# A two-layer decoder trunk on one core: trailing sums by scans, and second weight parts by a negation and an adding transfer

## The chip, the core and the metric

The kernel runs on one core of a Trainium2 chip. The number that counts is the device time of one execution in microseconds (us), median of three runs. Five engines take part, each with its own queue that is worked off in order: PE (TensorE, the matmuls), DVE (VectorE), ACT (ScalarE), POOL (GpSimd) and SP (SyncE, which here only issues transfers).

## The reference

The trunk has two layers, 1024 channels and 1024 tokens, all in float32. Each layer is a token mixer and then a squared-ReLU MLP with 4096 hidden channels; ahead of each stands an RMSNorm with a scale and a shift that come from a conditioning vector, and a last norm ends the trunk. Layer 0 mixes with a gated recurrence. Layer 1, which the change concerns, mixes with trailing means:

```python
def pool_mixer(h, w_pool, pool_scale):
    counts = jnp.arange(1, s + 1, dtype=jnp.float32)
    for g, win in enumerate((2, 4, 8, 16)):          # 4 groups of 256 channels
        xg = hf[..., g * 256:(g + 1) * 256]
        cs = jnp.cumsum(xg, axis=1)
        cs_lag = jnp.pad(cs, ((0, 0), (win, 0), (0, 0)))[:, :s]
        mean = (cs - cs_lag) / jnp.minimum(counts, float(win))[None, :, None]
        outs.append(mean - xg)
    mixed = jnp.einsum("bsgi,gij->bsgj", jnp.stack(outs, axis=2), w_pool)
    return mixed.reshape(bsz, s, 1024) * pool_scale

def sq_relu_mlp(h, w1, w2):
    u = jax.nn.relu(jnp.einsum("bsd,df->bsf", h, w1))
    return jnp.einsum("bsf,fd->bsd", u * u, w2)
```

## The kernel before

Channels lie on the 128 partitions, in eight blocks k; tokens lie along the free axis, in two halves of 512 (half 0 is `xa`, half 1 is `xb`). Matmuls take float32r operands. To keep float32 accuracy every operand is held in two parts that add up to it, and each product is three matmuls (`mm3`, L176 to L180): high weight by high data, high weight by low data, low weight by high data.

**Weights.** A unit of weights is a 128x1024 float32 tile that SP loads into `raw` (three buffers). `split_part` (L168 to L172) makes the two parts of a half unit of 512 columns: ACT copies it into the high part (L170), and DVE or POOL subtracts that from the raw tile (L171) into the low part. The tiles of parts come from a pool of eight, so ACT's copy for one half unit waits until PE has used the one eight places earlier. A half unit serves 12 matmuls.

**The MLP.** It is worked in chunks of 512 hidden channels, eight per layer. `f1` makes the hidden channels of a chunk, `f2` multiplies by the second matrix; `f2_fast` is a form of Strassen's for chunks of which both halves of tokens are there at once. After each block of `f1`, ACT takes the ReLU (L620), DVE squares it (L625), ACT casts the high part of `u` (L609) and DVE makes the low part (L610).

**The passage between the layers.** The second half of the program's work on the end of layer 0 and the start of layer 1 is written so that one half of the tokens has matmuls to do while the other half has norms and windows: `f1`, `f2` of the last chunk of layer 0 for half 0; then the windows of half 0 (`pool_windows`) beside the rest of `f2_fast` of chunk 6 and `f1` for half 1; `pool_mix` for half 0; `f2` of the last chunk for half 1, beside the norm for half 0's MLP (`ffn_norm`); the windows of half 1 beside layer 1's first chunk for half 0; `pool_mix` for half 1; and so on. Between these stand sums of squares over channels: ACT squares a block (L252), DVE (or POOL) adds it up (L253), PE sums over partitions (L262, `sm`), ACT takes the root (L265), DVE makes diagonals (`dg`, L274), PE spreads them (L276, `sm`). PE's rows for L262 and L276 stand at fixed places among its matmuls.

**The windows.** For each block k, DVE normalizes (`nt`, L880), ACT adds the shift into `hx` (L886), which holds 15 tokens of the half before ahead of its own 512. Blocks 0 and 1 (window 2) are a difference of neighbours (L939). The others add shifted copies, log2(window) times (`sums`, L900): blocks 2 to 5 on DVE, blocks 6 and 7 (window 16) on POOL, in advance. DVE then scales and subtracts (L907), mends the first 16 tokens of half 0 (L909, L910), ACT casts the high part (`ph`, L914) and DVE makes the low part (`pl`, L915). `pool_mix` multiplies these with the 256x256 matrices `w_p`, group by group, and DVE adds each block into x (L962).

The order of the instructions on each engine is set by a scheduler at build time, from the order in which the program is written, the dependencies and the free buffers; at run time each queue is strictly in that order. All temporaries of 512 tokens come from a pool of seven tiles (`tmp`), PSUM has six banks for products.

Of the kernel before, what the change touches and what calls it, by code (L numbers as in the profile page):

```python
# [15 lines left out]
P = 128  # L16
# [9 lines left out]
PAD = 15  # L26
W = PAD + H

# Columns of the packed per-channel vectors, eight columns (one per block of channels) each.
# [13 lines left out]
def trunk_kernel(ctx, tc, xT, vecs, wmod, w_k, w_in, w_y, w_g, w_out, w_p, w1, w2, outT):  # L43
# [16 lines left out]
    class Blocks:  # L60
        """Eight blocks of channels of one half of the tokens, in two slots"""
# [112 lines left out]
    def mm3(ps, unit, col, rh, rl, first, last):  # L174
        """ps += unit[:, col:col+128].T @ (rh + rl)"""
# [6 lines left out]
    def proj(unit, hh, hl):  # L182
        """One 128-row block of W.T @ h for one token half, K = 1024."""
# [11 lines left out]
    def mod_column(m, e, raw):  # L195
        """m[:, e] = raw @ cond"""
# [9 lines left out]
    def mod_steps():  # L206
        """The rest of the conditioning in small steps, taken between those of the other work."""
# [19 lines left out]
    def norm_scale(g, m, name):  # L227
        """g * (1 + scale)"""
# [5 lines left out]
    class SumSq:  # L234
        """Sums of squares of n tokens: up to three partial sums, added up by the tensor engine."""
# [19 lines left out]
    def rstd_bcast(ss, trace=None):  # L255
        """PSUM tile [P, n] with 1/sqrt(mean + eps) of every token on every partition."""
# [10 lines left out]
        # in two float32r parts on diagonals, whose sums over the partitions are on every partition  # L267
# [38 lines left out]
    # Six blocks of the input projection take the channels of the first half of the tokens  # L306
    # as the conditioning of each 128 of them is ready.
# [8 lines left out]
    def after(f, *args, **kw):  # L316
        """Issues behind what the last call on the same engine issued."""
# [7 lines left out]
    def column(dst, j, k, scale, first):  # L325
        """dst[:, k] = first + scale * (conditioning of channel block k)"""
# [16 lines left out]
    def prepare(q, part=0):  # L343
        """The float32r parts of the weights of two blocks of rows, or of one if q is 0"""
# [126 lines left out]
    # coefficient of the gate in log a: 8 * log_sigmoid(lambda)  # L471
# [17 lines left out]
    # log1p(z) = 2 s (1 + po)  # L489
# [11 lines left out]
    def gates(hd, unit, h):  # L501
        """RG-LRU of one head; its states take the place of its input."""
# [16 lines left out]
        for mi in range(2):  # L519
            b = 2 * hd + mi  # L520
            # a = exp(log a);  1 - a^2 = (1 + a^2) * tanh(-log a)
# [351 lines left out]
    def pool_windows(h, ss):  # L873
# [44 lines left out]
        for k in (6, 7):  # L918
            normed(k, hx16[:, k - 6, :])
# [193 lines left out]
```

## Time and profile before

| | |
|---|---|
| runs | 1798.16, 1798.73, 1800.46 us; median 1798.73 |
| span of the profiled execution, first to last instruction | 1797.3 us |
| PE busy | 1718.5 us (96%) |
| DVE busy | 1419.8 us (79%) |
| ACT busy | 913.7 us (51%) |
| POOL busy | 585.9 us (33%) |
| DMA engines, mean busy share | 26.9% |

The profile has no time of the profiled execution but its span; it stands 1.4 us under the median of the runs, and that much is taken to lie around it. Busy time counts an engine as busy while an instruction is in it; a PE row's duration is modelled, and the distance from one start to the next tells its pace. The granted clock (PEclk) is a share of full speed, where 1.0 is 2.4 GHz and 0.5 is 1.2 GHz.

### The profile page before, as it was taken

What the parts mean: (1) busy time and instruction counts of PE and PEld (TensorE: products, weight loads), DVE (VectorE), ACT (ScalarE), POOL (GpSimd) and SP (SyncE); (2) the same over time, 40 slices, a digit from 0 to 9 for tenths busy, and PEclk for the clock granted to TensorE, in tenths of its full rate; (3) what the DMA queues carried; (4) which work ended last, traced back from release to release, by engine and by line L of the source; (5) the groups of instructions that cost most, each with busy time, mean ns of one, the idle gap of its engine ahead of it and who ended that gap; (6) DMA issues with size and microseconds to landing.
All of it is one profiled execution on the core that took longest, in us unless ns stands there. A gap on an engine that the chain in (4) does not pass through costs nothing.

```text
span 1797.3 us, 20872 instructions
## 1 busy us (share of the span) xinstructions
PE 1718.5 (96%) x7510; PEld 1405.2 (78%) x7510; DVE 1419.8 (79%) x2124; ACT 913.7 (51%) x1558; POOL 585.9 (33%) x434
## 2 busy tenths in 40 slices
PE   6899989989999999999999988999999999999997
PEld 4687768778788888888888766788887787878787
DVE  8997866678888889898876897958787878686836
ACT  4588884255454444545454464445444444545422
POOL 5323341242322414151324655511322324041403
PEclk8999989989999999999999988999999999999999
DMA  9223314521424233242213221231202111121202
GB/s 363 73 84 109 136 47 142 162 83 59 136 70 134 73 115 106 94 126 73 83 58 106 81 72 59 83 105 51 70 33 71 36 59 52 42 61 46 71 13 94
DMA packets 47479, 158.76 MB, mean 88 GB/s; under 512 B 5008, under 2 KB 7440, under 8 KB 47376
## 3 DMA queue, kind: packets, MB, share of 16 engines
q1 hardware_dynamic: 47376, 157.43, 26.9%
q8 instruction: 59, 0.97, 0.2%
q14 instruction: 44, 0.36, 0.1%
HBM read 153.21 MB, written 4.19 MB: 88 GB/s over the span
## 4 chain that ended last, share of the span: by engine, by line
PE 62%; DVE 22%; ACT 5%; issue 5%; DMA 4%; POOL 2%; DVEq 0%; SPq 0%; ACTq 0%; POOLq 0%
PE mm L178 20%; PE mm L179 20%; PE mm L180 20%; DMA mb<-in_wmod 3%; DVE mb L197 2%; DVE xa L770 1%; DVE mw L323 1%; POOL xa L779 1%; DVE pw L900 1%; DVE xb L770 1%; DVE xca L439 1%; PE sm L262 1%; DVE hl L291 1%; DVE w_a_s L171 1%; DVE xcb L439 1%
## 5 line engine op out<-in xcount | busy, mean ns | idle before, releaser
L178 PE MATMUL mm<-hh,w_w 128*128 128x512 f32 x1024 | 401.4, 392 | 0.9 <-DVE xa L770 0.9
L180 PE MATMUL mm<-hh,w_w 128*128 128x512 f32 x1024 | 400.9, 392 | 0.0
L179 PE MATMUL mm<-hl,w_w 128*128 128x512 f32 x1024 | 400.6, 391 | 0.0
L779 POOL TENSOR_TENSOR xb<-xb,c 128x512 f32<-128x512 f32 x104 | 150.4, 1446 | 632.1 <-ACT c L774 564.4
L178 PEld LDWEIGHTS mm<-hh,w_w 128*128 128x128 f32 x1024 | 193.5, 189 | 42.8 <-DVE xa L770 2.7
L180 PEld LDWEIGHTS mm<-hh,w_w 128*128 128x128 f32 x1024 | 193.6, 189 | 40.3
L179 PEld LDWEIGHTS mm<-hl,w_w 128*128 128x128 f32 x1024 | 193.5, 189 | 40.0
L779 POOL TENSOR_TENSOR xa<-xa,c 128x512 f32<-128x512 f32 x104 | 160.3, 1542 | 145.1 <-ACT c L774 145.1
L774 ACT ACTIVATE c<-c,mod 128x512 f32<-128x512 f32 x104 | 75.3, 724 | 209.7 <-DVE c L800 119.8
L197 DVE SCALAR_TENSOR_TENSOR mb<-mb,cond 128x1024 f32<-128x1024 f32 x80 | 113.8, 1423 | 55.2 <-DMA mb<-in_wmod 54.6
L620 ACT ACTIVATE relu<-mm 128x512 f32<-128x512 f32 x128 | 76.2, 595 | 152.4 <-PE mm L180 143.6
L170 ACT CAST w_w<-raw_w 128x512 fp32r<-128x512 f32 x192 | 113.5, 614 | 63.2 <-PE mm L180 50.6
L171 DVE TENSOR_TENSOR w_w<-raw_w,w_w 128x512 fp32r<-128x512 f32 x136 | 130.5, 967 | 16.8 <-ACT w_w L170 16.7
L770 DVE SCALAR_TENSOR_TENSOR xa<-mm,mod,xa 128x512 f32<-128x512 f32 x156 | 112.9, 741 | 16.6 <-POOL xa L779 16.6
L171 POOL TENSOR_TENSOR w_w<-raw_w,w_w 128x512 fp32r<-128x512 f32 x56 | 83.5, 1498 | 71.6 <-ACT w_w L170 62.6
L179 PE MATMUL mm<-u,w_w 128*128 128x512 f32 (+1 forms) x224 | 81.4, 363 | 1.7 <-DVE u L610 1.7
L178 PE MATMUL mm<-u,w_w 128*128 128x512 f32 (+1 forms) x224 | 80.8, 364 | 1.7 <-ACT u L609 1.7
L180 PE MATMUL mm<-u,w_w 128*128 128x512 f32 (+1 forms) x224 | 81.0, 362 | 0.0
L178 PE MATMUL mm<-u,w_a_a 128*128 128x512 f32 x200 | 79.1, 396 | 1.9 <-DVE xa L770 1.0
L610 DVE TENSOR_TENSOR u<-usq,u 128x512 fp32r<-128x512 f32 x102 | 72.9, 715 | 8.5 <-ACT u L609 7.5
L770 DVE SCALAR_TENSOR_TENSOR xb<-mm,mod,xb 128x512 f32<-128x512 f32 x104 | 77.0, 741 | 2.6 <-PE mm L180 2.2
L179 PE MATMUL mm<-u,w_a_a 128*128 128x512 f32 x200 | 78.0, 390 | 0.0
(332 smaller groups left out, 4078.3 us busy)
## 6 DMA issues: line engine op xcount, KB each, us to landing
raw_w<-in_w SPq DMA_DIRECT2D x148, 512.0 KB, 3.6
mb<-in_wmod SPq DMA_DIRECT2D x80, 512.0 KB, 3.6
mw<-in_wmod SPq DMA_DIRECT2D x16, 512.0 KB, 9.6
raw_in<-in_w_in SPq DMA_DIRECT2D x8, 512.0 KB, 3.7
raw_y<-in_w_y SPq DMA_DIRECT2D x8, 512.0 KB, 3.6
raw_o<-in_w_out SPq DMA_DIRECT2D x8, 512.0 KB, 3.7
outT<-o SPq DMA_DIRECT2D x12, 256.0 KB, 2.4
xa<-in_xT SPq DMA_DIRECT2D x4, 512.0 KB, 5.4
```

What stands on the lines that cost most here:

```text
L170: S.copy(w[:, 0, 0:n], raw)
L171: (eng or V).tensor_sub(w[:, 1, 0:n], raw, w[:, 0, 0:n].bitcast(F32))
L178: PE.matmul(out=ps, lhsT=wh, rhs=rh, start=first, stop=False)
L179: PE.matmul(out=ps, lhsT=wh, rhs=rl, start=False, stop=False)
L180: PE.matmul(out=ps, lhsT=w[:, 1, c:c + P], rhs=rh, start=False, stop=last)
L197: V.scalar_tensor_tensor(raw, raw, 1.0, cond, op0=ALU.mult, op1=ALU.mult, accum_out=m[:, e:e + 1])
L439: V.scalar_tensor_tensor(o, xr[:, k:k + H], vcol(f"cw{k}", m), o, op0=ALU.mult, op1=ALU.add)
L610: eng.tensor_sub(u[n][:, 1, jj, :], src, u[n][:, 0, jj, :].bitcast(F32))
L620: S.activation(r, ps, AF.Relu)
L770: V.scalar_tensor_tensor(xb, ps, g[:, r + 4 * row:r + 4 * row + 1], xb, op0=ALU.mult, op1=ALU.add)
L774: S.activation(t, src, AF.Identity, scale=g[:, r + 4 * row:r + 4 * row + 1])
L779: G.tensor_add(xb, xb, t)
```

## The change

Two things are replaced, between the layers and at the start of layer 1.

**Trailing sums.** `sums` goes. `finish` runs one scan on DVE over a block: each element is the running sum plus the token that comes in, minus the token that leaves the window (add, then subtract). This holds for blocks 2 to 7, so that POOL no longer adds windows. The padding grows from 15 to 16 tokens. For half 0, ACT copies the last running sum of a block into `carry`, from which the scan of half 1 starts; the scaling by 1/window then writes over the running sums in place, so it stands behind that copy; and the first 16 tokens' products with 1/count are put in a small tile (`first`) ahead of it. The blocks are taken in the order 0 to 7, where blocks 6 and 7 went first.

**Second parts of weights.** `neg_part` replaces `split_part` for the units from `f1` of chunk 7, half 0, to `f2` of layer 1's chunk 0, half 1: 84 half units, 60 of whose low parts POOL made and 24 DVE. ACT copies the raw tile into the high part, then writes the negated high part into the low one; then POOL issues a transfer that reads the same half unit from memory again and adds it onto the low part.

```diff
+    def neg_part(raw, src, name):
+        w, n = split_tile(name), raw.shape[-1]
+        S.copy(w[:, 0, 0:n], raw)
+        S.activation(w[:, 1, 0:n], w[:, 0, 0:n].bitcast(F32), AF.Identity, scale=-1.0)
+        nc.gpsimd.dma_start(w[:, 1, 0:n], src, accum_op=ALU.add)
+        return w
+
     def split_unit(src, name, eng=None, drips=None):
         raw = load(src, name)
         drip(rate[0] if drips is None else drips)
+        if eng == "dma":
+            return [neg_part(raw[:, c:c + H], src[:, c:c + H], f"{name}_{c}") for c in (0, H)]
         return [split_part(raw[:, c:c + H], f"{name}_{c}", eng) for c in (0, H)]
...
-        def finish(k, hx, sm_, win):
-            d = tmp("pooled")
-            V.scalar_tensor_tensor(d, sm_, 1.0 / win, hx[:, PAD:W], op0=ALU.mult, op1=ALU.subtract)
+        def finish(k, hx):
+            win, d = WINDOWS[k // 2], tmp("pooled")
+            V.tensor_tensor_scan(d, hx[:, PAD:W], hx[:, PAD - win:W - win], 0.0 if h == 0 else carry[:, k:k + 1],
+                                 op0=ALU.add, op1=ALU.subtract)
             if h == 0:
-                V.tensor_mul(d[:, 0:16], sm_[:, 0:16], icnt[:, k // 2, :])
-                V.tensor_sub(d[:, 0:16], d[:, 0:16], hx[:, PAD:PAD + 16])
+                S.copy(carry[:, k:k + 1], d[:, H - 1:H])
+                first = mp.tile([P, 16], F32, tag="first", name="first", bufs=2)
+                V.tensor_mul(first, d[:, 0:16], icnt[:, k // 2, :])
+            V.scalar_tensor_tensor(d, d, 1.0 / win, hx[:, PAD:W], op0=ALU.mult, op1=ALU.subtract)
+            if h == 0:
+                V.tensor_sub(d[:, 0:16], first, hx[:, PAD:PAD + 16])
             split(k, d)
...
-        up = [split_unit(w_p[q], f"p{q}", G) for q in range(2)]
+        up = [split_unit(w_p[q], f"p{q}", "dma") for q in range(2)]
...
-    f1(0, 7, (0,))
-    f2(0, 7, (0,), sa)
+    f1(0, 7, (0,), eng="dma")
+    f2(0, 7, (0,), sa, eng="dma")
     side = pool_windows(0, sa)
-    f1(0, 7, (1,), eng=G, side=side)
+    f1(0, 7, (1,), eng="dma", side=side)
...
-    f2(0, 7, (1,), sb, eng=G, side=once(lambda: ffn_norm(1, 0, qa)))
+    f2(0, 7, (1,), sb, eng="dma", side=once(lambda: ffn_norm(1, 0, qa)))
     side = pool_windows(1, sb)
-    f1(1, 0, (0,), eng=G, side=side)
-    f2(1, 0, (0,), eng=G, side=side)
+    f1(1, 0, (0,), eng="dma", side=side)
+    f2(1, 0, (0,), eng="dma", side=side)
...
-    f1(1, 0, (1,), eng=G)
-    f2(1, 0, (1,))
+    f1(1, 0, (1,), eng="dma")
+    f2(1, 0, (1,), eng="dma")
```

Of the rest, `f2_weights_two` and `f1` of layer 1's chunk 1, half 0, change in the same way, and comments are gone, which shifts the line numbers.

The order on the engines moves at three places. First DVE, in the windows of half 0, one block of window 4 before (`pw` are the shifted sums, `usq` and `u` belong to the MLP's hidden channels):

```order
L880 SCALAR_TENSOR_TENSOR nt<-xa_82,amix_7305,sm 128x512
L883 MEMSET hx 128x15
L915 TENSOR_TENSOR pl_0_7953<-pooled,ph_0_7951 128x512
L900 TENSOR_TENSOR pw<-hx 128x526
L900 TENSOR_TENSOR pw<-pw 128x524
L907 SCALAR_TENSOR_TENSOR pooled<-pw,hx 128x512
L909 TENSOR_TENSOR pooled<-pw,icnt 128x16
L910 TENSOR_TENSOR pooled<-pooled,hx 128x16
L625 SCALAR_TENSOR_TENSOR usq<-mm,relu 128x512
```

The same place on DVE in the changed kernel; the scan is the row `pooled<-hx` of L905:

```order
L890 SCALAR_TENSOR_TENSOR nt<-xa_82,amix_7305,sm 128x512
L913 TENSOR_TENSOR pooled<-first,hx 128x16
L893 MEMSET hx 128x16
L905 SCALAR_TENSOR_TENSOR pooled<-hx 128x512
L918 TENSOR_TENSOR pl_0_7971<-pooled,ph_0_7969 128x512
L910 TENSOR_TENSOR first<-pooled,icnt 128x16
L911 SCALAR_TENSOR_TENSOR pooled<-pooled,hx 128x512
L635 SCALAR_TENSOR_TENSOR usq<-mm,relu 128x512
```

One scan stands where two shifted additions stood (three for window 8), and the scaling has moved behind ACT's copy into `carry`.

Then ACT, at the same stage, where the weights `w_p` of `pool_mix` are made between the steps of the windows, before:

```order
L170 CAST w_p_0_8297<-raw_p_8295 128x512
L888 COPY tail<-hx 128x15
L890 COPY hx<-hx 128x1
L886 ACTIVATE hx<-nt,mod_0_3550 128x512
L914 CAST ph_0_7951<-pooled 128x512
```

and in the changed kernel:

```order
L163 CAST w_p_0_8313<-raw_p_8311 128x512
L896 ACTIVATE hx<-nt,mod_0_3550 128x512
L908 COPY carry<-pooled 128x1
L164 ACTIVATE w_p_0_8313<-w_p_0_8313 128x512
L898 COPY tail<-hx 128x16
L163 CAST w_p_512_8317<-raw_p_8311 128x512
L164 ACTIVATE w_p_512_8317<-w_p_512_8317 128x512
L917 CAST ph_0_7969<-pooled 128x512
```

Each copy of weights has a negation (L164) behind it, and between two steps of the windows there are now two or three ACT instructions on weights where there was one.

Last PE, where the sum of squares for half 0's MLP norm is taken among the matmuls of `f2`, before (u is the hidden data, `w_w_0_7_1_512` the second half of `f2`'s second unit):

```order
L180 MATMUL mm<-u_8101,w_w_0_7_1_512_8503 128x512
L262 MATMUL sm<-ones,ssqf1aV 128x1 x4
L178 MATMUL mm<-u_8101,w_w_0_7_1_512_8503 128x512
L179 MATMUL mm<-u_8101,w_w_0_7_1_512_8503 128x512
L180 MATMUL mm<-u_8101,w_w_0_7_1_512_8503 128x512
```

and in the changed kernel, where the row stands behind the first unit:

```order
L190 MATMUL mm<-u_8098,w_w_0_7_0_512_8424 128x512
L272 MATMUL sm<-ones,ssqf1aV 128x1 x4
L188 MATMUL mm<-u_8097,w_w_0_7_1_0_8522 128x512
L189 MATMUL mm<-u_8097,w_w_0_7_1_0_8522 128x512
L190 MATMUL mm<-u_8097,w_w_0_7_1_0_8522 128x512
```

The row stood behind 39 matmuls of `f2` and stands behind 24. Else PE's order is the same but for a few rows that change places.

## Rows read from the trace of the kernel before

**Rows 1.** Windows: busy us (instructions) per engine, granted clock, DMA share, GB/s.
```profile
core 0: us, PE busy (x) PEld busy (x) DVE busy (x) ACT busy (x) POOL busy (x), PEclk, DMA share, GB/s
900.00:950.00 50.00, 50.00 (x222) 41.32 (x222) 40.53 (x60) 28.35 (x51) 16.51 (x12) 1.00 0.17 56
1005.00:1155.00 150.00, 131.51 (x523) 104.05 (x522) 132.53 (x177) 74.39 (x141) 88.69 (x60) 0.90 0.23 73
1200.00:1250.00 50.00, 50.00 (x222) 41.45 (x221) 38.16 (x66) 23.73 (x42) 3.12 (x3) 1.00 0.23 72
```

**Rows 2.** Waits of PE from 990 to 1160 us: who, total us, times, longest.
```profile
PE mm L178 <- DVE usq L625: 4.9, 1, 4.9
PE sm L262 <- DVE ssqn0bV L253: 4.4, 1, 4.4
PE mm L178 <- ACT ph L914: 1.9, 1, 1.9
PE mm L179 <- DVE u L610: 1.7, 1, 1.7
PE mm L178 <- DVE xa L962: 1.7, 2, 1.5
PE mm L178 <- ACT u L609: 1.7, 1, 1.7
PE sm L262 <- DVE ssqf1aV L253: 0.9, 1, 0.9
```

**Rows 3.** Timeline of PE: start, duration, instruction, [idle before, releaser].
```profile
1005.11 0.39 PE L178 MATMUL mm<-hh,w_w 128*128 128x512 f32 x1
1007.83 0.39 PE L178 MATMUL mm<-hh,w_w 128*128 128x512 f32 x1
...
1035.97 0.80 PE L178 MATMUL mm<-ph,w_p 128*128 128x512 f32 x1 [4.86 <-DVE usq L625]
1036.57 0.63 PE L179 MATMUL mm<-pl,w_p 128*128 128x512 f32 x1
1036.99 0.63 PE L180 MATMUL mm<-ph,w_p 128*128 128x512 f32 x1
...
1060.24 1.02 PE L262 MATMUL sm<-ones,ssqf1aV 128*128 128x1 f32 x8 [0.88 <-DVE ssqf1aV L253]
...
1063.53 0.39 PE L276 MATMUL sm<-dg,ones_r 128*128 128x512 f32 x1
...
1155.71 0.95 PE L262 MATMUL sm<-ones,ssqf1bV 128*128 128x1 f32 x8
```

**Rows 4.** Groups on DVE from 1010 to 1060 us: busy, mean ns, idle before.
```profile
L900 DVE TENSOR_TENSOR pw<-pw 128x524 f32<-128x524 f32 (+1 forms) x6 | 8.4, 1407 | 0.2
L253 DVE TENSOR_TENSOR ssqf1aV<-ssqf1aV,sq 128x512 f32<-128x512 f32 x7 | 6.6, 949 | 0.0
L962 DVE SCALAR_TENSOR_TENSOR xa<-mm,gp,xa 128x512 f32<-128x512 f32 x8 | 5.9, 742 | 1.2 <-PE mm L180 1.2
L915 DVE TENSOR_TENSOR pl<-pooled,ph 128x512 fp32r<-128x512 f32 x8 | 5.7, 726 | 0.2 <-ACT ph L914 0.2
L907 DVE SCALAR_TENSOR_TENSOR pooled<-pw,hx 128x512 f32<-128x512 f32 x6 | 5.4, 920 | 0.1
L900 DVE TENSOR_TENSOR pw<-hx 128x526 f32<-128x526 f32 x4 | 4.8, 1196 | 0.1
```

**Rows 5.** All instructions of one operation: durations min/median/max in ns, first and last start.
```profile
L536 DVE TENSOR_TENSOR_SCAN xca<-a,gate x8: 1196/1208/1218, 151.1 to 252.3; 128x512 f32<-128x512 f32 x8
L171 DVE TENSOR_TENSOR w_w<-raw_w,w_w x136: 673/693/1783, 456.6 to 1739.1; 128x512 fp32r<-128x512 f32 x136
L171 POOL TENSOR_TENSOR w_w<-raw_w,w_w x56: 1262/1346/2378, 348.8 to 1175.8; 128x512 fp32r<-128x512 f32 x56
```

**Rows 6.** Groups on ACT from 1000 to 1160 us, columns as in 4.
```profile
L170 ACT CAST w_w<-raw_w 128x512 fp32r<-128x512 f32 x37 | 22.5, 617 | 22.2 <-PE mm L180 20.3 <-issue 0.9 <-POOL pwork L900 0.9
L886 ACT ACTIVATE hx<-nt,mod 128x512 f32<-128x512 f32 x12 | 8.6, 722 | 1.7 <-DVE nt L880 1.7
L170 ACT CAST w_p<-raw_p 128x512 fp32r<-128x512 f32 x8 | 4.7, 615 | 2.4 <-PE mm L180 2.4
```

**Rows 7.** Transfers: issue on SP's queue (ns), and KB each, us to landing.
```profile
L99 SPq DMA_DIRECT2D raw_w<-in_w x96: 327/328/372, 330.6 to 1707.2; - x96
raw_w<-in_w SPq DMA_DIRECT2D x4, 256.0 KB, 2.8
kr<-in_w_k SPq DMA_DIRECT2D x1, 512.0 KB, 10.2
q1 hardware_dynamic: 47376, 157.43, 26.9%
```

**Rows 8.** Timeline of DVE around the windows of half 0: start, duration, instruction.
```profile
1005.98 1.41 DVE L880 SCALAR_TENSOR_TENSOR nt<-xa,amix,sm 128x512 f32<-128x512 f32 x2
...
1020.50 0.18 DVE L910 TENSOR_TENSOR pooled<-pooled,hx 128x16 f32<-128x16 f32 x1
...
1047.44 0.68 DVE L915 TENSOR_TENSOR pl<-pooled,ph 128x512 fp32r<-128x512 f32 x1
```

More of the change, by code (lines that the diff above doesn't have):

```diff
@@ L25 @@
 WINDOWS = (2, 4, 8, 16)
-PAD = 15
+PAD = 16
 W = PAD + H
@@ L744, in f2_weights_one, with f2_weights_two @@
         return {1: (wa, 0, (0, 0)), 3: (wa, 256, (1, 1)), 5: (wb, 256, "t1"), 6: (wb, 0, "t2"), 7: (wc, 0, "t3")}
-    def f2_weights_two(i, c, r, eng):
+    def f2_weights_two(i, c, r):
         raw = rawp.tile([P, D + 256], F32, tag="raw", name=f"raw_w2_{i}_{c}_{r}")[:, 0:H]
         nc.sync.dma_start(raw, w2[i, c, r, :, 256:768])
-        w = split_part(raw, "a12_a22", eng)
+        w = neg_part(raw, w2[i, c, r, :, 256:768], "a12_a22")
         return {2: (w, 0, (1, 0)), 4: (w, 256, "t4")}
@@ L890, in normed @@
                     S.copy(hx[:, PAD - 1:PAD], hx[:, PAD:PAD + 1])
-        def sums(hx, win, eng, work=None):
-            cur, n = hx, 0
-            step = 1
-            while step < win:
-                if work is None or 2 * step == win:
-                    nxt = tmp("pw", W)
-                else:
-                    nxt = work[:, step.bit_length() % 2, :]
-                eng.tensor_add(nxt[:, n + step:W], cur[:, n + step:W], cur[:, n:W - step])
-                cur, n = nxt, n + step
-                step *= 2
-            return cur[:, PAD:W]
-        def finish(k, hx, sm_, win):
-            d = tmp("pooled")
-            V.scalar_tensor_tensor(d, sm_, 1.0 / win, hx[:, PAD:W], op0=ALU.mult, op1=ALU.subtract)
-            if h == 0:
-                V.tensor_mul(d[:, 0:16], sm_[:, 0:16], icnt[:, k // 2, :])
-                V.tensor_sub(d[:, 0:16], d[:, 0:16], hx[:, PAD:PAD + 16])
+        def finish(k, hx):
+            win, d = WINDOWS[k // 2], tmp("pooled")
+            V.tensor_tensor_scan(d, hx[:, PAD:W], hx[:, PAD - win:W - win], 0.0 if h == 0 else carry[:, k:k + 1],
+                                 op0=ALU.add, op1=ALU.subtract)
+            if h == 0:
+                S.copy(carry[:, k:k + 1], d[:, H - 1:H])
[4 more added lines that the diff above has]
+                V.tensor_sub(d[:, 0:16], first, hx[:, PAD:PAD + 16])
             split(k, d)
@@ L915, in split @@
             V.tensor_sub(lo[:, k, :], d, hi[:, k, :].bitcast(F32))
-        hx16 = slot("hx", (2, W))
-        for k in (6, 7):
-            normed(k, hx16[:, k - 6, :])
-        work = slot("pwork", (2, W))
-        late = [(k, hx16[:, k - 6, :], sums(hx16[:, k - 6, :], 16, G, work), 16) for k in (6, 7)]
         hxs = {}
         def ahead(k):
-            if k < 6:
+            if k < NB:
                 hxs[k] = tmp("hx", W)
@@ L933, in pool_windows @@
         yield
-        for k in range(6):
+        for k in range(NB):
             ahead(k + 2)
@@ L941, in pool_windows @@
             else:
-                win = WINDOWS[k // 2]
-                finish(k, hx, sums(hx, win, V), win)
-            if k == 4:
-                for args in late:
-                    finish(*args)
-            if k != 0:
+                finish(k, hx)
+            if k % 2 or k == 2:
                 yield
@@ L976, in trunk_kernel @@
     f2_fast(0, 6, Ahead([partial(f2_weights_one, 0, 6, r, V) for r in range(4)]), (1, 5, 6, 3, 7))
-    f1(0, 7, (0,))
-    f2(0, 7, (0,), sa)
+    f1(0, 7, (0,), eng="dma")
+    f2(0, 7, (0,), sa, eng="dma")
     side = pool_windows(0, sa)
-    f2_fast(0, 6, Ahead([partial(f2_weights_two, 0, 6, r, G) for r in range(4)]), (2, 4), side)
-    f1(0, 7, (1,), eng=G, side=side)
+    f2_fast(0, 6, Ahead([partial(f2_weights_two, 0, 6, r) for r in range(4)]), (2, 4), side)
+    f1(0, 7, (1,), eng="dma", side=side)
     for _ in side:
@@ L991, in trunk_kernel @@
     pool_mix(1, pooled[1], qb)
-    f1(1, 1, (0,), eng=G, side=once(lambda: ffn_norm(1, 1, qb)), fast="in turn")
-    f1(1, 0, (1,), eng=G)
-    f2(1, 0, (1,))
+    f1(1, 1, (0,), eng="dma", side=once(lambda: ffn_norm(1, 1, qb)), fast="in turn")
+    f1(1, 0, (1,), eng="dma")
+    f2(1, 0, (1,), eng="dma")
     ahead = Ahead(jobs(1, 1, 7))
```

## The prediction

> **What bounds the kernel now.** I read the busy times in long windows first. Before and after the passage between the layers PE is busy all the time at full clock: 50.00 of 50 us with 222 matmuls, twice [rows 1]. Only the passage, 1005 to 1155 us, falls out: 131.5 of 150 us busy, granted clock 0.90, while DVE is busy 132.5, ACT 74.4 and POOL 88.7 us [rows 1]. So a change can win in this passage alone, and I first ask how much is lost there. At full pace PE starts a matmul every (1007.83 - 1005.11) / 12 = 0.227 us [rows 3]. From the first matmul of `f1` at 1005.11 to the sum for half 1's MLP norm at 1155.71 [rows 3] there are 504 of them in the order (21 groups of 24), 114.2 us, and with two sums and two spreads of about 1.5 us together each, 117.3. The trace takes 150.6. **Lost: 33.3 us**, and no change in this passage can win much more.
>
> The waits of PE tell to whom it is lost: 17.2 us in seven rows, nearly all on DVE or on ACT steps that DVE releases [rows 2]. The other half is pace: after the 4.86 us wait at 1036, matmuls start 0.42 us apart, not 0.227 [rows 3]; the engine has dropped from 2.4 to 1.2 GHz after idling. A wait of 0.88 us in front of the sum at 1060.24 is the small kind [rows 2, 3]. Hence a wait that vanishes also takes its slow stretch along.
>
> The reason is a DVE backlog. In the windows of half 0 DVE runs from 1006 to 1048.1 with hardly an idle moment [rows 4, 8], and PE stands in front of `pool_mix` because the squares of `f1`, queued between windows, free their PSUM banks late (the 4.9 us row, released by `usq`) [rows 2]. The later waits (sums `ssqf1a`, `ssqn0b`, then `u`, `ph`) are the same backlog carried on.
>
> **The scans, and DVE freed from POOL.** Removed for half 0 on DVE: ten shifted additions, 8.4 + 4.8 = 13.2 us [rows 4]. Added: six scans. The kernel's own scans of 128x512 take 1.21 us [rows 5], so 7.3 us; they mix other operations, and the nearest other rows are 0.69 (one plain pass) and 1.78 (the slowest subtraction) [rows 5], which bounds the six at 4.1 and 10.7. I take 1.21, the same instruction. POOL's 16 additions of windows go too, and its subtractions of weights with them. That matters to DVE: the same subtraction takes 0.69 at the median and up to 1.78 [rows 5], and in the windows L907 stands at 0.92 and the adds of squares at 0.95 [rows 4]. At 0.69 the six L907 give 1.4 back, and the small mending steps, the differences and L915 about as much twice over, 4.2 us in all (below 0 there is no reason; 0 if the slow ones had another cause). DVE also no longer has four x updates (L962, 0.74 each) and one add of squares (0.69), 3.7 us, ahead of the last `pl`, since these stand behind it in the new order. So the last `pl` comes at 1048.1 - 13.2 + 7.3 - 4.2 - 3.7 = 1034.3. PE reaches `pool_mix` at 1005.11 + 96 x 0.227 = 1026.9, and its last group after 36 more, 1035.0. It need not wait. The banks are free as well, as the squares move up with the windows.
>
> **The copy into `carry`.** The scaling in place now waits for an ACT copy of one column, and DVE's whole queue waits behind it. ACT is at most one weight pair behind, 0.62 + 0.72 us [rows 6]; the scheduler puts other DVE work between scan and scaling. I count nothing, at most 6 x 1.3 = 8 us.
>
> **The negations on ACT.** In the passage ACT makes 37 + 8 = 45 copies of half units [rows 6]; each gets a negation, 0.62 (as a copy) to 0.72 us (as the shifted `hx`) [rows 6], 28 to 32 us, and 1 us for `carry`. ACT goes from 74.4 to about 105 us, in a passage of some 127: 83%. That hides only if its order fits, since ACT waits 22.7 us for PE to free a tile of weights [rows 6] and then everything behind it waits. I follow it at the four handovers. The sum `ssqf1a` now stands 15 matmuls earlier: PE is there at 1026.9 + 72 x 0.227 = 1043.2. DVE needs from 1034.3 eight updates and seven adds, 8 x 0.74 + 7 x 0.69 = 10.7 us, so 1045.0; ACT in the same time eight squares and four weight pairs, about 10.4. **Wait 2 us.** The spread that follows waits 1.5 (nine matmuls, 2.0 us, for root, reciprocal and diagonals, which took 3.3 before [rows 3]). The sum `ssqn0b` comes 22 us later, and its backlog is gone: 1 us for its spread. The hand-over of `u` from `f1` to `f2` keeps a chain of ReLU, square, cast, subtraction, each 0.6 to 0.7: 1.5 us. Ahead of 1005 ACT makes 20 more negations in slack (28 of 50 us busy [rows 1]); 1.5 us for the first norm's last square, which now stands behind a weight pair. Some slow pace after these, 2.5. **Left over: 10 us.** Their ends: 3 if all hide, 20 if each costs twice that.
>
> **The adding transfers.** There are 84, one per half unit, and PE uses a half unit in 12 x 0.227 = 2.72 us. The raw tile no longer has to wait for a subtraction, and the tiles are made up to seven half units ahead (19 us), so the landing is covered: 2.8 us for a plain 256 KB load, and even the slowest, 10.2 [rows 7], would be. No row shows an issue from POOL or a transfer that adds. From below, SP's issue takes 0.33 us [rows 7]; the subtraction that POOL now does in its place takes 1.35 at the median and 2.38 at most [rows 5]. I take 1.35 and count nothing, as it is under 2.72; the far end is one transfer at a time, 0.33 + 2.8 = 3.1, which is a rival below. The bytes: 84 x 262 KB = 22 MB in some 230 us, 96 GB/s beside 73 at a share of 0.23 [rows 1]: 0.53, or 0.83 if an adding byte costs double. It holds.
>
> On the price of an issue from POOL the Trainium skill speaks against the change: its page "SBUF — State Buffer" (section "A bandwidth-pool intuition that's wrong") says that GpSimd cannot write the descriptors while VectorE holds both port pairs, and that a transfer of about 620 ns then took 3100. By 3.1 us each the passage would come out where it was. Its case is a plain VectorE copy, and the groups that fill DVE's passage here are two-input steps [rows 4]; so I give it little.
>
> **Sum.** 33.3 - 10 = 23.3 us off the profiled span of 1797.3: 1774.0, and with the 1.4 us by which the runs' median stands above it, 1775.4; I say **1776**.
>
> **Rivals.**
> *ACT becomes the bound.* For: 83% busy in strict order, and copies that wait for PE stand between the windows' steps. Against: when PE is ahead, those waits shrink. If every handover waits 3 us more (four of them) and drops the clock for as long, 10 to 12 us more are lost: 1787. The same time comes out if the scans cost 1.78 and the DVE list ends 3.4 us later, with the sums behind it.
> *POOL cannot issue fast enough, the other side.* Up to 2.72 us per transfer nothing shows. From there PE runs at POOL's pace through 84 half units, 228 us at full speed. Before, the passage took 33 more, so the turning point is (228 + 33) / 84 = 3.1 us each, above it the kernel is slower: at 3.5 us, 294 - 261 = 33 us slower, 1832. For: nothing in the trace has this form; one transfer at a time gives just 3.1. Against: eight tiles of weights let transfers overlap, and POOL has little else to do.
> *Nothing moves.* The transfers at 3.1 us (the page's rule, or one at a time), or a backlog that merely moves from DVE to ACT whole: 1798.
>
> **How the numbers follow.** Forecast 0.62, between 1768 and 1784. ACT as bound 0.20, 1784 to 1795. POOL too slow 0.09, above 1802. Nothing moves 0.05. Better than 1768 (nearly all the loss gone) 0.04. The range 1768 to 1793 leaves out the last three and the end of the second, 2 in 10. A measurement can tell about 0.2% here, 3.6 us: faster than that 0.86, within it 0.05, slower 0.09.
>
> **What would show it.** In the changed profile: the clock between 1005 and 1130 near 1.00 and PE's waits on `usq` and `ssqn0b` gone; the last `pl` of half 0 near 1034; scans at 1.2 us and L907's successor at 0.69; ACT above 80% in the passage; the sum `ssqf1b` near 1132, not 1155.7; no wait of PE on a low part. Wrong would be: PE waiting in front of the third matmul of a product (a low part late: POOL or the landing), scalings that wait for `carry`, or ACT busy without a gap while PE's sums wait.

## The result, and the profile after

The changed kernel takes 1766.34 us (median of four runs, 1764.47 to 1767.23); beside it the kernel before took 1798.45. The ratio is 0.9819, with a 95% interval from 0.9805 to 0.9833: 32 us faster. The forecast was faster, 1776, with a range from 1768 to 1793; the time lies 1.7 us below that range.

The first view is the windows of the changed kernel, columns as in [rows 1]; the first row ends just ahead of the sum for half 1's MLP norm.

```profile
...
1005.00:1124.00 119.00, 118.89 (x531) 98.01 (x530) 103.41 (x169) 97.07 (x188) 41.28 (x46) 1.00 0.87 186
1005.00:1155.00 150.00, 149.89 (x672) 123.78 (x671) 120.25 (x192) 123.44 (x236) 53.84 (x59) 1.00 0.85 183
1200.00:1250.00 50.00, 50.00 (x222) 41.42 (x221) 44.76 (x71) 25.30 (x46) 19.53 (x14) 1.00 0.21 64
```

In the stretch where PE was busy 131.51 of 150 us at a clock of 0.90 [rows 1], it is now busy 149.89 at 1.00. The view of PE's waits, which had 17.2 us in seven rows [rows 2] and 1.8 us more in three small ones not shown there, has not one row between 940 and 1160 us. Ahead of the passage and behind it PE works as before (50.00 of 50 us, 222 matmuls). So the whole gain lies where the prediction looked for it.

The timeline of PE in the changed kernel: the first matmul of `f1` for half 1, the first of `pool_mix`, the sum and the first spread for half 0's MLP norm, the sum for half 1's MLP norm. None has an idle time in brackets.

```profile
1006.25 0.39 PE L188 MATMUL mm<-hh,w_w 128*128 128x512 f32 x1
...
1028.01 0.39 PE L188 MATMUL mm<-ph,w_p 128*128 128x512 f32 x1
...
1044.34 0.95 PE L272 MATMUL sm<-ones,ssqf1aV 128*128 128x1 f32 x8
1047.32 0.40 PE L286 MATMUL sm<-dg,ones_r 128*128 128x512 f32 x1
...
1124.03 0.95 PE L272 MATMUL sm<-ones,ssqf1bV 128*128 128x1 f32 x8
```

From 1006.25 to 1124.03 are 117.8 us. The 504 matmuls, two sums and two spreads at full pace are 117.3 by the prediction; before, they took 150.6 [rows 3]. Of the 33.3 us lost, 32.8 are back. The passage begins 1.1 us later than before (1006.25 for 1005.11). That is scatter from the start of the program, not work of the change: the first product's first matmul starts at 20.24 us where it was 19.06, and in a second trace of the changed kernel (the run `a1_after` below) it starts at 19.09 and the passage at 1005.36, with the same 117.8 us to its end. So the end moves up by 1155.71 - 1124.03 = 31.7 us; the span went from 1797.3 to 1765.1, 32.2.

DVE's timeline around the end of half 0's windows: the last two low parts `pl` (the second ends at 1031.24), the last add of squares ahead of the sum at 1044.34, and the diagonals ahead of the spread at 1047.32:

```profile
1029.86 1.38 DVE L918 TENSOR_TENSOR pl<-pooled,ph 128x512 fp32r<-128x512 f32 x2
...
1042.48 0.69 DVE L263 TENSOR_TENSOR ssqf1aV<-ssqf1aV,sq 128x512 f32<-128x512 f32 x1 [0.54 <-ACT sq L262]
...
1046.12 0.69 DVE L284 TENSOR_TENSOR dg<-ident,rstdh 128x512 fp32r<-128x512 f32 x1
```

Before, the last `pl` ended at 1048.1 [rows 8], 43.0 us after the first matmul of `f1`; now it is 25.0 us after it. The squares are added up at 1043.17, 1.2 us before PE comes for them, and the first diagonals are there at 1046.81, 0.5 us before PE comes for those. The handovers are close, and PE still finds each of them done.

The groups on DVE from 1010 to 1060 us, columns as in [rows 4]:

```profile
L905 DVE TENSOR_TENSOR_SCAN pooled<-hx 128x512 f32<-128x512 f32 x6 | 7.2, 1210 | 0.0
L955 DVE SCALAR_TENSOR_TENSOR xa<-mm,gp,xa 128x512 f32<-128x512 f32 x8 | 5.9, 744 | 0.0
...
L263 DVE TENSOR_TENSOR ssqf1aV<-ssqf1aV,sq 128x512 f32<-128x512 f32 x7 | 4.8, 684 | 0.8 <-ACT sq L262 0.8
...
L911 DVE SCALAR_TENSOR_TENSOR pooled<-pooled,hx 128x512 f32<-128x512 f32 x6 | 4.0, 688 | 0.1
...
```

The scans cost 1.21 as the kernel's own did. L911 (L907 before) went from 920 to 688 ns, the adds of squares from 949 to 684. The x updates, with an operand in PSUM, stand at 744 where they stood at 742 [rows 4].

Last ACT's weights from 1000 to 1160 us, as in [rows 6]; the issues on POOL with the durations of all (min/median/max in ns) and their landing; and the queues (packets, MB, share of 16 engines over the whole span) with the plain loads of 256 KB, as in [rows 7]:

```profile
L164 ACT ACTIVATE w_w<-w_w 128x512 fp32r<-128x512 f32 x49 | 30.9, 630 | 1.0
L163 ACT CAST w_w<-raw_w 128x512 fp32r<-128x512 f32 x49 | 30.1, 614 | 10.9 <-PE mm L190 10.9
...
```
```profile
L165 POOL DMA_DIRECT2D w_w<-in_w x72: 852/872/1667, 938.7 to 1165.9; - x72
...
DMA to landing us min/median/max: 3.8/5.6/8.3
```
```profile
q1 hardware_dynamic: 47376, 157.43, 27.7%
q0 software_dynamic: 12096, 22.03, 7.5%
...
raw_w<-in_w SPq DMA_DIRECT2D x4, 256.0 KB, 5.1
```

A negation costs 0.63 us; ACT's waits for PE in front of a copy fall from 20.3 us [rows 6] to 10.9, with 49 copies in place of 37. An issue takes POOL 0.87 us at the median and the landing 5.6. The four plain loads of the same size took 2.8 before [rows 7] and take 5.1 now, beside DMA engines that are busier: so the adding alone does not make the difference.

### The profile page after: what moved, and what is told of

Read it like the earlier page. It is cut to its first block, busy times and chain, and to the rows that moved or that the text cites. A ratio compares the mean times of both kernels' runs of the same rounds, so it can differ in the third digit from the quotient of the medians.

```text
span 1765.1 us, 20959 instructions
## 1 busy us (share of the span) xinstructions
PE 1704.2 (97%) x7510; PEld 1397.7 (79%) x7510; DVE 1367.9 (77%) x2092; ACT 959.7 (54%) x1648; POOL 544.3 (31%) x442
## 3 DMA queue, kind: packets, MB, share of 16 engines
q1 hardware_dynamic: 47376, 157.43, 27.7%
q0 software_dynamic: 12096, 22.03, 7.5%
## 4 chain that ended last, share of the span: by engine, by line
PE 71%; DVE 15%; ACT 5%; DMA 4%; issue 3%; POOL 1%; SPq 0%; DVEq 0%; ACTq 0%; POOLq 0%
PE mm L188 23%; PE mm L189 23%; PE mm L190 23%; DMA mb<-in_wmod 3%; DVE mb L207 2%; DVE mw L333 1%; DVE xca L449 1%; DVE xa L780 1%; PE sm L272 1%; DVE xb L780 1%; POOL xa L789 1%; DVE xcb L449 1%; DVE hl L301 1%; DVE nt L294 1%; POOL asq L538 1%
## 5 line engine op out<-in xcount | busy, mean ns | idle before, releaser
L181 DVE TENSOR_TENSOR w_w<-raw_w,w_w 128x512 fp32r<-128x512 f32 x112 | 108.5, 977 | 12.0 <-ACT w_w L180 11.7
L165 POOL DMA_DIRECT2D w_w<-in_w x72 | 63.9, 906 | 106.6 <-ACT w_w L164 65.9
L180 ACT CAST w_w<-raw_w 128x512 fp32r<-128x512 f32 x120 | 69.8, 612 | 27.9 <-PE mm L190 20.6
L188 PE MATMUL mm<-u,w_a_a 128*128 128x512 f32 x200 | 79.1, 396 | 2.2 <-DVE xa L780 1.0
L189 PE MATMUL mm<-u,w_a_a 128*128 128x512 f32 x200 | 78.0, 390 | 0.0
L190 PE MATMUL mm<-u,w_a_a 128*128 128x512 f32 x200 | 77.9, 389 | 0.0
```

Source lines behind the costliest of these rows:

```text
L165: nc.gpsimd.dma_start(w[:, 1, 0:n], src, accum_op=ALU.add)
L180: S.copy(w[:, 0, 0:n], raw)
L181: (eng or V).tensor_sub(w[:, 1, 0:n], raw, w[:, 0, 0:n].bitcast(F32))
L188: PE.matmul(out=ps, lhsT=wh, rhs=rh, start=first, stop=False)
L189: PE.matmul(out=ps, lhsT=wh, rhs=rl, start=False, stop=False)
L190: PE.matmul(out=ps, lhsT=w[:, 1, c:c + P], rhs=rh, start=False, stop=last)
```

## The experiments

Each kernel was timed beside the kernel before; its ratio to that is given with its 95% interval. The theories: **P**, the gain is POOL's arithmetic gone, which had stretched DVE's instructions; **S**, the gain is fewer DVE passes through the scans; and the prediction's own rivals, ACT and POOL's issues as bounds.

**The two parts apart.** First the scans alone: the changed kernel with POOL and DVE subtracting as before.

```diff
-    f1(0, 7, (1,), eng="dma", side=side)
+    f1(0, 7, (1,), eng=G, side=side)
...
```

> The trailing sums by scans as in the changed kernel, the second parts of the weights subtracted on POOL and DVE as before. Theory P (the gain comes from POOL's arithmetic no longer stretching DVE's instructions: before, a shifted add took 0.69 us where POOL stood idle and 1.6 to 1.7 where it subtracted): POOL still subtracts 60 half units, so scaling and mending stay stretched (L911 near 0.9 us on average in the windows of half 0), PE still waits 8 to 12 us there and the time is 1783 to 1792. Theory S (the gain comes from the fewer DVE passes, ten adds of 1.2 to 1.4 us against six scans of 1.21): 1766 to 1773, as the changed kernel.

Measured: 1783.17 us, ratio 0.9906 (0.9891 to 0.9921), 16 us faster than before and 17 slower than the changed kernel. PE's longest waits in the passage, and DVE's groups from 1005 to 1060 us:

```profile
PE sm L272 <- DVE ssqf1aV L263: 4.8, 1, 4.8
PE mm L188 <- ACT u L619: 2.3, 1, 2.3
...
```
```profile
L263 DVE TENSOR_TENSOR ssqf1aV<-ssqf1aV,sq 128x512 f32<-128x512 f32 x7 | 8.0, 1148 | 0.2
L905 DVE TENSOR_TENSOR_SCAN pooled<-hx 128x512 f32<-128x512 f32 x6 | 7.2, 1204 | 0.0
...
L955 DVE SCALAR_TENSOR_TENSOR xa<-mm,gp,xa 128x512 f32<-128x512 f32 x8 | 5.8, 740 | 0.0
L911 DVE SCALAR_TENSOR_TENSOR pooled<-pooled,hx 128x512 f32<-128x512 f32 x6 | 5.1, 850 | 0.0
...
L913 DVE TENSOR_TENSOR pooled<-first,hx 128x16 f32<-128x16 f32 x6 | 2.0, 340 | 0.0
```

Then the transfers alone: the kernel before with `neg_part` in all places of the change, and its shifted adds kept.

```diff
-    f1(0, 7, (1,), eng=G, side=side)
+    f1(0, 7, (1,), eng="dma", side=side)
...
```

> The second parts of the weights by negation and adding transfer as in the changed kernel, the trailing sums by shifted adds as before (blocks 6 and 7 on POOL). Theory P: with POOL idle but for its 16 adds, the DVE adds fall from 1.2 to 1.4 us to about 0.7 (ten of them 7 us, less than six scans), L907 to 0.69, PE waits under 4 us between 1005 and 1130, time 1766 to 1774. Theory S: the ten adds keep 1.2 us or more each and the DVE list of half 0 stays some 6 us longer than in the changed kernel, time 1780 to 1790.

Measured: 1767.96 us, ratio 0.983 (0.9811 to 0.9848), 31 us faster than before. PE's waits, and the same DVE code as in [rows 4], from 1005 to 1050 us:

```profile
PE mm L187 <- ACT u L618: 1.8, 1, 1.8
PE sm L271 <- DVE ssqn0bV L262: 0.8, 1, 0.8
PE mm L187 <- DVE xa L971: 0.4, 1, 0.4
```
```profile
L262 DVE TENSOR_TENSOR ssqf1aV<-ssqf1aV,sq 128x512 f32<-128x512 f32 x7 | 4.8, 681 | 0.0
L909 DVE TENSOR_TENSOR pw<-pw 128x524 f32<-128x524 f32 (+1 forms) x6 | 4.2, 700 | 0.1
...
L909 DVE TENSOR_TENSOR pw<-hx 128x526 f32<-128x526 f32 x4 | 2.8, 700 | 0.1
```

This is the reading that decides. The ten shifted adds, 13.2 us in [rows 4], take 7.0 with not a line of them changed. Six scans take 7.2. Theory S falls for DVE's passes: a scan replaces two or three adds that, left alone, cost no more than it. Theory P holds: the transfers alone bring 31 of the 32 us (29 when timed again below).

How POOL does it stands in the run with scans alone, in the timelines of POOL and of DVE:

```profile
1040.37 1.29 POOL L181 TENSOR_TENSOR w_w<-raw_w,w_w 128x512 fp32r<-128x512 f32 x1 [1.45 <-ACT w_w L180]
```
```profile
1040.43 1.78 DVE L263 TENSOR_TENSOR ssqf1aV<-ssqf1aV,sq 128x512 f32<-128x512 f32 x1
1042.13 0.74 DVE L955 SCALAR_TENSOR_TENSOR xa<-mm,gp,xa 128x512 f32<-128x512 f32 x1
1042.79 0.68 DVE L263 TENSOR_TENSOR ssqf1aV<-ssqf1aV,sq 128x512 f32<-128x512 f32 x1
```

The add that starts 0.06 us after POOL's subtraction ends 0.55 us after it, as if DVE stood until POOL was nearly through and only then worked. The add 2.4 us later, with POOL idle, takes 0.68. It hits instructions that read two SBUF operands (adds, subtractions, L911, and the 128x16 mends at 340 for 170 ns), not those with an operand in PSUM (L955 at 740). The Trainium skill says this: "SBUF — State Buffer", section "SBUF: two separate sides", has DVE and GpSimd share one pair of ports as an exclusive lock, for DVE with two SBUF inputs against a GpSimd instruction that reads SBUF. The trace agrees, 1.78 for 0.68 us. It also shows one small cast with a single operand that was hit (L279, 128x4, 0.80 for 0.17 us).

Scans are no exception. In the same run POOL's subtraction starts inside a scan of half 0 and runs long; in half 1 a scan starts inside a subtraction and runs long itself; the last row is a scan of half 1 with POOL idle:

```profile
1019.05 2.04 POOL L181 TENSOR_TENSOR w_p<-raw_p,w_p 128x512 fp32r<-128x512 f32 x1 [2.09 <-ACT w_p L180]
```
```profile
1018.79 1.20 DVE L905 TENSOR_TENSOR_SCAN pooled<-hx 128x512 f32<-128x512 f32 x1
```
```profile
1094.09 1.29 POOL L181 TENSOR_TENSOR w_w<-raw_w,w_w 128x512 fp32r<-128x512 f32 x1 [2.29 <-ACT w_w L180]
```
```profile
1094.91 1.56 DVE L905 TENSOR_TENSOR_SCAN pooled<-hx,carry 128x512 f32<-128x512 f32 x1
...
1110.33 1.27 DVE L905 TENSOR_TENSOR_SCAN pooled<-hx,carry 128x512 f32<-128x512 f32 x1
```

Whoever started first kept its time here. In half 0 no scan of this run began with more than 0.03 us of a subtraction left, so all six kept 1.20 to 1.22 us; in half 1 the three that began inside one took 1.53 to 1.56, the other three 1.27.

Why then are the scans alone worth 16 us? They take POOL's 16 additions of windows away too, and by the luck of order no scan of half 0 was stretched: 1204 ns beside POOL's subtractions, 1210 without. Both single kernels end half 0's windows at almost the same time, the last `pl` at 1037.1 with scans alone and at 1036.5 with the transfers alone (31.9 and 33.2 us after the first matmul of `f1`). What differs comes behind it: seven adds of squares at 1148 against 681 ns, so that the sum waits 4.8 us in one and not at all in the other. Part of that is the sum's place in PE's order, 16 matmuls or 3.6 us earlier with scans alone. The two parts overlap: 16 and 31 make more than the 32 of both.

**What the scans add.** The changed kernel and the one with the transfers alone were timed again beside each other.

> The changed kernel again, beside the two next ones on the same chip: 1764 to 1768.

> Negation and adding transfer alone, trailing sums by shifted adds, once more with more rounds. If the scans are worth nothing once POOL's subtractions are gone (ten adds of 0.70 us against six scans of 1.21): within 1 us of the changed kernel. If POOL's 16 additions of windows still stretch DVE and the handover of u keeps its wait of 1.8 us: 1.5 to 3 us slower than the changed kernel.

Measured: 1766.31 us (1764.28 to 1767.52) and 1769.0 us (1767.42 to 1769.74), ratios 0.9816 (0.9801 to 0.9832) and 0.9831 (0.9816 to 0.9846). The medians differ by 2.7 us, by 1.6 in the first pair; the intervals overlap. Within the passage the traces show more. From the first matmul of `f1` to the sum `ssqf1b` the two traces of the transfers alone take 123.0 and 121.3 us, both traces of the changed kernel 117.8. So the scans, with the order that comes with them, are worth 3.5 to 5.2 us there, 3.0 of which are the waits that the first of these traces has left. Why the medians show only 1.6 to 2.7 was not followed up.

**Is ACT near its limit?** The changed kernel with each negation made twice.

```diff
         S.activation(w[:, 1, 0:n], w[:, 0, 0:n].bitcast(F32), AF.Identity, scale=-1.0)
+        S.activation(w[:, 1, 0:n], w[:, 0, 0:n].bitcast(F32), AF.Identity, scale=-1.0)
```

> The changed kernel with each negation made twice on ACT: 84 more ACT instructions of 0.63 us, about 45 of them between 1000 and 1124 us, where ACT is busy about 101 of 125 us; it would need 129. Theory that ACT is close to being the bound (the rival of the prediction): 10 to 25 us slower than the changed kernel, 1776 to 1792, with PE waiting for sums, ReLU or weights behind ACT. Theory that ACT has room because it only waited for tiles that PE frees: within 4 us of it, 1764 to 1770.

Measured: 1771.57 us, ratio 0.9844 (0.9829 to 0.9858), 5 us slower than the changed kernel, between the two expectations. The window of the passage and PE's waits from 940 to 1160 us:

```profile
1005.00:1127.00 122.00, 121.59 (x541) 99.76 (x540) 105.42 (x172) 118.19 (x239) 41.56 (x46) 1.00 0.85 183
```
```profile
PE mm L189 <- ACT u L620: 2.5, 1, 2.5
...
PE sm L287 <- DVE dg L285: 0.4, 1, 0.4
```

ACT is busy 97% of the passage and PE waits 0.4 us in it. The 5 us are lost ahead of it, at 950 to 1005, where the 2.5 us stand and PE starts 229 matmuls in place of 251. So within the passage ACT at 82%, in a strict order and with close handovers, was not near a bound; ahead of it there is less room. That what ACT does for PE is worked off ahead, up to the tiles that PE frees, would explain it; no run tests that.

**How near is POOL's queue?** The adding transfers cut in two, by columns in one kernel and by partitions in another.

```diff
-        nc.gpsimd.dma_start(w[:, 1, 0:n], src, accum_op=ALU.add)
+        for c in (0, n // 2):
+            nc.gpsimd.dma_start(w[:, 1, c:c + n // 2], src[:, c:c + n // 2], accum_op=ALU.add)
```

> The changed kernel with each adding transfer cut into two of 256 columns: 168 issues on POOL, the same bytes. If an issue costs 0.87 us whatever its size, POOL takes 1.74 us per half unit, under the 2.72 us in which PE uses one: 1764 to 1770. If the transfers themselves are what has little room (DMA engines 0.81 to 0.93 busy in the passage, and rows of 1 KB cost more than half of rows of 2 KB): PE waits in front of the third matmul of a product, and the time is 1775 or more.

Measured: 1815.45 us, ratio 1.0091 (1.0074 to 1.0107), slower than the kernel before.

```diff
-        nc.gpsimd.dma_start(w[:, 1, 0:n], src, accum_op=ALU.add)
+        for p in (0, P // 2):
+            nc.gpsimd.dma_start(w[p:p + P // 2, 1, 0:n], src[p:p + P // 2], accum_op=ALU.add)
```

> The changed kernel with each adding transfer cut into two of 64 partitions by 512 columns: 168 issues, the same bytes and rows of 2 KB as in the uncut one, where the cut by columns made 1815 us with POOL standing 44 us before issues for nothing that the trace shows. If a fixed number of transfers may be under way, whatever their size: the same standing, 1795 or more. If a fixed number of rows may be: no standing, POOL takes 1.74 us per half unit or less, 1764 to 1772.

Measured: 1767.94 us, ratio 0.9825 (0.9808 to 0.9841), within 2 us of the changed kernel. The cut by columns: PE's longest waits from 930 to 1240 us, then POOL's standing before issues (us, times) and the landing from 900 to 1200:

```profile
PE sm L273 <- POOL ssqn0aG L264: 12.5, 1, 12.5
PE mm L191 <- DMA w_w<-in_w: 7.8, 6, 2.5
PE mm L190 <- POOL hl L299: 5.0, 2, 3.1
...
```
```profile
  issue: 44.4, 29
...
DMA to landing us min/median/max: 3.0/4.6/7.2
```

POOL's standing in the cut by partitions, where PE has one wait of 0.9 us and one of 0.2:

```profile
  issue: 0.9, 3
```

The queue of POOL's transfers over the whole span, cut by columns and then by partitions:

```profile
q0 software_dynamic: 24192, 22.03, 8.2%
```
```profile
q0 software_dynamic: 13440, 22.03, 7.6%
```

Both have 168 issues and the same bytes. "issue" is time in which POOL stood before a transfer for nothing that the profile shows: 44.4 us in 29 places in one, 0.9 in the other. What differs is the packets: 144 per half unit in the changed kernel (12096 / 84), 288 cut by columns, 160 cut by partitions. So the number of transfers is not the limit; the rows fit a bound on packets under way, which no run here measured by itself. Rows of 1 KB where there were 2 KB are a rival that these two runs do not part from it. Either way it is not the 0.87 us of an issue from which POOL decides here: at twice the packets the kernel is slower than before, as PE waits for what else POOL does behind its issues (`ssqn0aG`, `hl`) and for low parts that come late (`w_w`, 7.8 us).

**POOL's arithmetic put back for nothing.** POOL also subtracts two pieces of each raw half unit into columns that nobody reads.

```diff
                 w.append(neg_part(raw[:, c:c + H], src[:, c:c + H], f"{name}_{c}"))
+                for _ in range(2):
+                    G.tensor_sub(raw[:, D:D + 256], raw[:, c:c + 256], raw[:, c + 256:c + H])
```

> The changed kernel with POOL arithmetic put back that nobody needs: behind each adding transfer of a unit (80 of the 84) POOL subtracts two pieces of 128x256 of the raw tile into its spare columns, about 1.3 us, as long as the subtraction that the change took away. Theory P (POOL's arithmetic stretches DVE's two-input instructions while it runs, and that was the loss): L911 in the windows of half 0 rises from 0.69 to about 0.85 us and the adds of squares to 1.1, as in the run with scans alone, while the scans keep 1.20; PE waits 5 to 12 us for DVE; 1775 to 1786. Rival (what cost time was who makes the low part and when, not the work beside DVE): DVE's durations may rise, the time stays at 1764 to 1769.

Measured: 1811.65 us, ratio 1.0065 (1.0048 to 1.0082). DVE's groups from 1020 to 1062 us and PE's longest wait:

```profile
L915 DVE TENSOR_TENSOR_SCAN pooled<-hx 128x512 f32<-128x512 f32 x6 | 7.2, 1207 | 0.0
L921 DVE SCALAR_TENSOR_TENSOR pooled<-pooled,hx 128x512 f32<-128x512 f32 x6 | 6.9, 1155 | 0.1
...
```
```profile
PE sm L282 <- POOL ssqn0aG L273: 11.2, 1, 11.2
...
```

The stretching came as Theory P has it, and more (1155 ns where 850 were expected), with the scans at 1207 again. The time says less than it seems: 11.2 us are POOL's own sum of squares that stands behind the added work in its queue, beside 17.8 us of waits for DVE where 5 to 12 were expected, and the raw tiles are held longer. As a measure of the price of contention this run is spoilt; the two parts apart give that. The rival, late low parts, is answered by the trace of before: no wait of PE there stands in front of a third matmul of a product (L180), the one that reads a low part of weights [rows 2].

**Fewer and more transfers.** The adding transfer only for the 60 half units that POOL had subtracted, and, in another kernel, also for 16 half units earlier on.

> The changed kernel with the negation and adding transfer only for the 60 half units that POOL subtracted before; the 24 others (chunk 7 of layer 0 for half 0, second product of layer 1's chunk 0 for half 1) go back to DVE's subtraction. DVE has room at both places (22.7 of 55 us busy from 950 to 1005, 14.4 of 30 from 1130 to 1160): the same within 2 us, 1764 to 1768. If the sums for the first norm come earlier because ACT has 16 negations less, up to 1 us faster; if the DVE subtractions push those sums back, 2 to 5 us slower.

Measured: 1765.26 us, ratio 0.981 (0.9796 to 0.9825).

> The changed kernel with the adding transfer only for the 60 half units that POOL subtracted before, once more with more rounds. If the 24 others are of no use: within 1 us of the changed kernel. If their 16 negations ahead of 1005 us hold up the first norm: 1 to 2 us faster than it.

Measured: 1765.72 us (1764.66 to 1768.39), ratio 0.9816 (0.98 to 0.9832), beside 1766.31 for the changed kernel. The 24 half units of DVE gain nothing and cost nothing that can be measured.

> The changed kernel, and the same way of making second parts also for the 16 half units that POOL subtracts around 330 to 450 us (first half of the output projection, first MLP chunk of layer 0), where PE is busy 91.7 of 100 us (300 to 400) and waits 4.9 us for POOL's sums of squares. Theory P: less arithmetic on POOL there brings these sums and DVE's steps earlier, 3 to 8 us faster than the changed kernel, 1758 to 1763. Rival: the waits there are a chain of norm steps that has nothing to do with POOL's subtractions, 1764 to 1769.

Measured: 1767.26 us, ratio 0.9818 (0.9803 to 0.9832). No gain: PE's wait for POOL's sums there is 5.8 us where it was 4.9. Theory P's 3 to 8 us did not come, so those waits are not a queue behind POOL's subtractions. No kernel of the study is clearly faster than the changed one.

**Plain copies on DVE beside POOL's issues.** The high parts of the last 24 half units copied by DVE.

> The changed kernel with the high parts of its last 24 half units copied by DVE, not ACT, so that plain DVE copies run beside POOL's issues between 1130 and 1200 us, where DVE is busy 14 of 30 us. By the rows of the changed kernel, where DVE was busy 28 to 29 of 30 us with two-input instructions and an issue took 0.86 to 0.89: the issues keep 0.87 and the time 1764 to 1769. If a plain DVE copy holds up the issue as long as it runs or longer: issues above 1.3 us at those places and, with up to 24 of them, no change in time either as long as they stay under 2.72 us; above it 1770 or more. [...]

Measured: 1764.79 us, ratio 0.981 (0.9792 to 0.9828). DVE's copies, then POOL's issues from 1120 to 1180 us (min/median/max):

```profile
L163 DVE CAST w_w<-raw_w x24: 407/424/452, 1102.4 to 1161.5; 128x512 fp32r<-128x512 f32 x24
```
```profile
L165 POOL DMA_DIRECT2D w_w<-in_w x17: 862/875/982, 1120.2 to 1164.5; - x17
```

A copy takes 0.42 us, and no issue beside it more than 0.98. An issue at 1136.81 took 0.88 while three copies ran from 1136.33 to 1137.41. The landing took 6.6 us at the median from 1120 to 1180, against 5.8 in the changed kernel; whether the copies or the closer spacing of the issues does that is open.

## Why the prediction was wrong, point by point

**Where the loss was: right.** 33.3 us in one passage, half of it waits and half slow pace after them, and no more to be had: 32.8 of them went. The prediction named this outcome (nearly all the loss gone) and gave it 0.04. That a wait takes its slow stretch along is seen in the granted clock from 1005 to 1124 us: 0.96 with scans alone and some 10 us of waits, 0.99 with the transfers alone and 3.0, and 1.00 in the changed kernel with none.

**The scans and DVE freed from POOL: near in sum, wrong in the parts.** The prediction took ten adds at 13.2 us against six scans at 7.3, a gain of 5.9, and gave the contention 4.2. But 1.41 and 1.20 us were not the price of a shifted add; they were contention. Without POOL the adds take 0.70 (transfers alone), so the scans give DVE nothing (7.0 to 7.2) and the contention 6.2 more. The row that showed it stood in the trace of before, the same subtraction at 0.69 and 1.78 [rows 5]; it was read for one group and not for the one that carried the largest term. Nor did the forecast ask which instructions are hit: the x updates with their PSUM operand at 742 ns stood beside the adds of squares at 949 [rows 4]. The Trainium skill's section "SBUF: two separate sides" (page "SBUF — State Buffer") says which, and was not put to use.

**The end of the windows: too late by 4.2 us.** Traces start up to 3 us apart, so count from the first matmul of `f1`: the last `pl` came after 43.0 us before, was forecast after 29.2 and came after 25.0. The contention alone brings it to 33.2 (transfers alone), 9.8 us where adds, L907 and mends together had been given 5.9 + 4.2 = 10.1: near in sum by luck, since all of it is contention. Scans, order and moved updates bring the other 8.2, where 3.7 had been given. How these divide was not measured.

**Left over: the step that failed.** It was put at 10 us, 3 if all hid; it is 117.8 - 117.3 = 0.5. Term by term:

- The wait of 2 us at `ssqf1a` came from the windows' end. PE came there at 1044.34, 72 matmuls after 1028.01 as worked out, but DVE was done at 1043.17: 36.9 us after the first matmul of `f1`, not 39.9. Measured: no wait.
- The 1.5 us at the spread were a misreading. The 3.3 us "before" run from the start of the sum to the start of the spread and hold the sum's own 1.0, which the 2.0 us of the nine matmuls do not. Taken alike, the same stretch takes 2.98 in the changed kernel with no wait in it (1044.34 to 1047.32). Root, reciprocal and diagonals take from 1045.29 to 1046.81, 1.5 in all; before they took 2.0, with a stretched add ahead of the reciprocal.
- `ssqn0b` (1 us), the handover of `u` (1.5), the first norm's last square (1.5) and the slow pace (2.5) were allowances with no row of a wait outside the backlog behind them. All four are nothing.

The range's lower end stood at 1768 for the same reason, and even with all hidden (3 us left, 1768.4) the sum would have stood 2 us too high.

**ACT: size right, rival wrong.** 83% forecast, 97.07 of 119 us measured, 82%. As a bound it was given 1787 and 0.20; with 97% the kernel still makes 1771.57. The 1787 was also added up short: four waits of 3 us are the 12, and the clock that drops for as long would come on top.

**The copy into `carry`: right.** The scaling L911 waits 0.1 us in all.

**The issues: right on the side, not on the size.** 0.87 us where 1.35 was taken, below the turning point of 3.1. That there is a point from which POOL makes the kernel slower held, by another mechanism: the rows point to the number or size of the packets, not the issue's own time. The Trainium skill's 3100 ns ("SBUF — State Buffer", section "A bandwidth-pool intuition that's wrong") are those of a whole transfer held up beside a copy, and the prediction took them for the price of an issue. No issue came near them: 1667 ns was the longest in the changed kernel, 982 beside plain DVE copies of 0.42 us.

**The bytes: the second reading.** The share was put at 0.53, or 0.83 if an adding byte costs double. It is 0.87 in the passage. From the queues' rows: 22.03 MB at 7.5% of 1765.1 us, 132 us, make 166 GB/s; 157.43 MB at 27.7%, 489 us, make 322. By these rows an adding byte costs 1.9 times a loaded one, and the loads, too, come faster now that PE does not wait. It held, with less room than thought.

## What to carry to other kernels

Before an operation is priced by its mean row, look at its minimum and maximum: where the same shape takes 0.69 and 1.7 us, the difference may belong to another engine, as here, and taking that engine's work away frees every instruction that it hit, not only the one that is rewritten. When a change removes the cause of a backlog, size what is left from rows outside the backlog, since the handovers inside it are late for the same cause, and measure both sides of a handover from the same start. And arithmetic on POOL beside a busy DVE is not free work; handing it to ACT and to DMA engines with room was worth 29 to 31 us here, while the scans alone, which also took POOL's window additions away, were worth 16.

## What the runs showed of the hardware that was not expected

- Between a scan and a subtraction on POOL the one that started first kept its time. POOL's subtraction took 2.04 us when it began 0.26 us into a scan, at a least time of 1.27; a scan took 1.53 to 1.56 us when it began inside a subtraction, for 1.27 otherwise.
- Adding transfers move 166 GB/s of busy time on the DMA engines where loads move 322, and land in 5.6 us; plain loads of the same size land in 5.1 in the same kernel, in 2.8 in the one before.
- Two transfers of half the columns cost far more than two of half the partitions: 1815 against 1768 us at the same bytes and the same number of issues.
